# A hybrid decoder layer on one core: first loads, a deferred store, two PSUM tiles, an earlier block load and a halved last store

## The chip, the cores and the metric

The kernel runs on one core of one Trainium2 chip. The metric is the time of one launch in microseconds (us) of device time; three runs of the kernel before gave 2040.29, 2042.28 and 2039.11 us, so its median is 2040.29 us. A core has five engines, each with its own instruction stream: PE (TensorE, matrix products into the PSUM memory), DVE (VectorE), ACT (ScalarE), POOL (GpSimd) and SP (SyncE, which here only issues DMA transfers). PEld is PE's weight load, which overlaps its products. "SPq" and "POOLq" in a profile are the issuing of DMAs on SP and on POOL.

## The reference, cut to what matters

The input is 512 tokens of width 2048, with 16 learned meta tokens set in front. All arithmetic is float32.

```
n = rmsnorm(h) * g_mix;  q, k, v, gb, gc, u = split(n @ w_in)
o_attn = stick_breaking_attention(norm(q), norm(k), v)       # 8 heads of 128
o_conv = gb * causal_dwconv3(gc * u)                         # 1024 channels
h = h + concat(rmsnorm(o_attn), rmsnorm(o_conv)) @ w_out
n2 = rmsnorm(h) * g_ffn
h = h + (silu(n2 @ w_gate) * (n2 @ w_up)) @ w_down           # 5632 wide
return h[meta tokens dropped]
```

## The kernel before, in words

Everything is kept transposed: a tile has 128 channels on its partitions and the tokens along its rows. The matmuls take float32r operands. For float32 accuracy each weight block and each activation block is split into a high and a low part of that type, and a product is three matmuls: high by high, high by low, low by high. The split of a weight block is a CAST on ACT (line 188, the high part) and a subtraction on DVE (line 189, the low part), from the load buffer `w_buf` into the split buffer `s_buf`, which has three places (four for the smaller blocks).

The stages follow one another, and PE is fed without a break from one to the next:

- **The head.** SP issues the vector of gains `vec` (line 72), then by turns pieces of the first weight columns (`load_at`, line 172) and the 16 tiles of x (`load_x`, line 345). Ten small matmuls on ones (line 85) keep PE busy while the loads are under way. `split_x` makes `nh` (ACT, line 351) and `nl` (DVE, line 352) of each x tile, and the k and q products of the first attention head start as soon as the first tile and the first weight piece are split.
- **Attention heads and convolution.** Then comes the rest of w_in.
- **The output projection.** 16 output tiles, of which each takes an attention half (activations `oa`) and a convolution half (`oc`). Each output tile has one PSUM tile `po` with two banks: bank 0 for the attention half, bank 1 for the other (lines 848 to 850 are the three matmuls). In the last two output tiles the attention halves of both are computed first, `attention_half` (line 907) has DVE read bank 0 of each, and only then the convolution halves follow.
- **Gate and up.** 44 pairs (`f`), each computed by `pair_product` in seven block products instead of eight: the blocks x, z, x, z, x, y, x, with y first in the first pair. Between them ACT copies partial sums from PSUM to `sides` (lines 769, 772 and 775), and DVE forms outputs (lines 778, 783 and 788). The third copy, `u2` of line 775, reads x, into which the fifth block (the third on x) then accumulates, so PE must wait for it. `gate` works on the results of a pair while the next pair runs: for even f two combined blocks, for odd f five (`odd`), which `store_acts` splits (ACT and DVE, lines 294 and 295, 1280 columns for odd f) and stores to DRAM as `fd`.
- **Down.** The 22 double blocks of `fd` are taken in four chunks of 4, 6, 6 and 6. For chunk 0 the loop over `j` has four passes of four output tiles; for each later chunk eight passes of two. Each chunk needs seven activation blocks, s = 0 to 6, loaded from `fd` by POOL into `first` (chunk 0) or `ring` (the later chunks). The block products use s = 0, 1, 2, 3, 4, 5, 6 in this order. While chunk 0 is computed, chunk 1 is loaded: blocks 0 and 1 in the second pass, 2 and 3 in the third, 4 and 5 in the fourth, and block 6 in the middle of the fourth, when its place comes free. A load of a block is two DMAs, the high part and the low part, of 768 KB each. So that the loads come no earlier, a tiny POOL operation (line 1074, "TENSOR_SCALAR ring<-d") writes into the place from `last`, an output of the pass before, and the DMAs wait for it. POOL also adds each finished output to DRAM (`add_down`, line 1113, an accumulating DMA "out_T<-d"). In the last chunk the last two output tiles are finished on the core (lines 1170 to 1176) and stored by SP.

A scheduler orders each engine's instructions by priority and by estimated times; `in_turn` stamps some instructions with a token so that they keep the order in which they are written. Each DMA of POOL takes the next of eight semaphores in turn, so that it waits until the DMA eight before it has landed.

Of the kernel before, what the change touches and what calls it, by code (L numbers as in the profile page):

```python
# [33 lines left out]
def hybrid_layer(ctx: ExitStack, tc: tile.TileContext, xT, w_in, w_out, w_gu, w_down, vecs, out):  # L34
# [36 lines left out]
    vec = keep.tile([P, 75], F32, name="vec")  # L71
    nc.sync.dma_start(vec, vecs)
    sc.preload_act_table_set("natural_log_exp_and_others")
# [109 lines left out]
    def split_quad(src, n, turn=False):  # L183
# [6 lines left out]
        split_w.append((hi, lo, n))  # L190

    def in_turn(inst, on=True):
        if on:
            tc.stamp_issue_order_token(inst.ins, "first_pairs")
# [97 lines left out]

    def split(hi, lo, src, eng=ve):
        sc.copy(hi, src)
        eng.tensor_tensor(lo, src, hi.bitcast(F32), ALU.subtract)  # L295
# [73 lines left out]
    for i, (a, b) in enumerate(FIRST):  # L369
        for m in range(2):  # L370
            load_at(HEAD_PLACES[2 * i + m])
            for k in range(len(xts), (a + b) // 2 if m == 0 else b):
                load_x(k)
    for place in HEAD_PLACES[2 * len(FIRST) :]:
        load_at(place)
# [370 lines left out]
    def pair_product(acts, c1, c2, sides, m=1, fourth=None, second=None):  # L746
# [27 lines left out]
        with tc.high_priority(1 << 20):  # L774
            sc.copy(u2, x)  # L775
        block_product(z, acts[3], False, m)
# [115 lines left out]
    def run(steps):  # L892
        for _ in steps:
            pass
# [16 lines left out]
    for i, j in enumerate(OUT_TILES):  # L911
# [5 lines left out]
        if i < KT - 2:  # L917
            hj = attention_half(i, gp if half else ve)
        elif i == KT - 2:
            hs = [attention_half(m, ve) for m in (i, i + 1)]  # L920
        if i >= KT - 2:
            hj = hs[i - KT]
            run(wide_product(ps_out[i][:, 1, :], oc))
        ps = ps_out[i]
        t2 = wide_tmp("t2")
# [4 lines left out]
        def residual(eng):  # L930
            ve.tensor_tensor(t2, ps[:, 1, :], acc_c, ALU.mult)
            eng.tensor_tensor(hj, hj, t2, ALU.add)
            sc.activation(src[:, 2 * half : 2 * half + 2], two(hj), AF.Copy, scale=g_ffn[:, j : j + 1])
# [101 lines left out]

    def store_acts(blks, n, slots, kp):

        t = apool.tile([P, 2, n, T2], F32R, tag=f"s{n}", name=f"s{kp}_{n}")
        split(t[:, 0], t[:, 1], blks)
        c, k = at[kp]  # L1040
        for i, s in enumerate(slots):
            if kp < FT // 2 - 1:
                gp.dma_start(fd[c][s][:, :, k], t[:, :, i])  # L1043
            else:
                nc.sync.dma_start(fd[c][s][:, :, k].bitcast(F32), t[:, :, i].bitcast(F32))
# [3 lines left out]
    def gate(f, g1, u1, x):  # L1049
# [8 lines left out]
        else:  # L1058
# [5 lines left out]
            ve.scalar_tensor_tensor(odd[:, 4], odd[:, 3], -1.0, odd[:, 0], ALU.mult, ALU.subtract)  # L1064
            store_acts(odd, 5, (5, 6, 1, 2, 3), f // 2)

# [64 lines left out]
    for j in range(KT // 4):  # L1131
        for s in ((0, 1), (2, 3), (4, 5))[j - 1] if j else ():
            load_acts(1, s, last)
        c1, c2 = (d, d2)[j % 2][:, 0:2], (d, d2)[j % 2][:, 2:4]
# [13 lines left out]
    for c in range(1, len(CHUNKS)):  # L1148
        end = c == len(CHUNKS) - 1
        for j in range(KT // 2):  # L1150
# [18 lines left out]
            if last_pair:  # L1169
                ve.tensor_tensor(c2, c2, r_h, ALU.mult)  # L1170
                ve.tensor_tensor(c2, c2, h2[1], ALU.add)
                nc.sync.dma_start(two(out[2 * j + 1]), c2)
                ve.tensor_tensor(c1[:, 0], c1[:, 0], r_h[:, 0], ALU.mult)
                ve.tensor_tensor(c1[:, 0], c1[:, 0], h2[0][:, 0], ALU.add)
                ve.tensor_tensor(c1[:, 1], x, r_h[:, 1], ALU.mult)  # L1175
                ve.tensor_tensor(c1[:, 1], c1[:, 1], h2[0][:, 1], ALU.add)  # L1176
                nc.sync.dma_start(two(out[2 * j]), c1)
            else:
                first_sums(2 * j, c1, x, 1)
# [62 lines left out]
```

## Time and profile before

| | |
|---|---|
| median of three runs | 2040.29 us (2039.11 to 2042.28) |
| the profiled execution | 2040.52 us, of which the span from the first to the last instruction is 2038.8 us |
| mean granted TensorE clock over the span | 0.999 |
| HBM traffic | 278.50 MB read, 80.61 MB written |
| DMA q0 (POOL's queue) and q1 (SP's) | 129.65 MB and 229.51 MB |

How to read the lines of the timeline: start in us, duration in us, engine, line of the kernel, operation, "out<-in", the engine's operands and the count of merged instructions; in brackets, how long the engine had been idle and what ended that. A matmul's duration is longer than the distance to the next one, since matmuls are pipelined; the pace is read from start to start. The rows of stages (windows) give the stage, its length, the busy time and count of each engine, the granted PE clock, the mean busy share of the 16 DMA engines (over 1 where transfers overlap) and GB/s. Rows of waits give the engine and line, what it waited for, the total us, the times and the longest. Rows of DMA issues give the transfer, the queue, the count, the size and the time from issue to landing in us.

### The profile page before, as it was taken

The numbers are of one execution on the slowest core, as the hardware profiler recorded it, in microseconds if no ns is written. First come the engines' busy times: TensorE is split into PE (matmuls) and PEld (weight loads), VectorE is DVE, ScalarE is ACT, GpSimd is POOL, SyncE is SP. The second block draws the span as 40 slices with busy tenths as digits, with TensorE's granted clock in tenths as the row PEclk, the third lists the DMA queues.
The fourth block names the chain that finished last, engine by engine and source line by source line (L and its number), as shares of the span: only waits on it lengthen the run. The fifth ranks groups of instructions, "written<-read, shape, count | busy, mean of one in ns | idle before, by whom it ended". The sixth has DMA issues, their size and how long they took to land.

```text
span 2038.8 us, 39740 instructions
## 1 busy us (share of the span) xinstructions
PE 2028.3 (99%) x16158; PEld 1966.2 (96%) x16158; DVE 1721.0 (84%) x2202; ACT 1049.4 (51%) x1517; POOL 381.2 (19%) x532
## 2 busy tenths in 40 slices
PE   9999999999999999999999999999999999999999
PEld 8999999999998889999999999999999999999999
DVE  8788878588977779989989989989989888888887
ACT  7666666344444436455555555555555544444443
POOL 0111111210015440111110110110110252222111
PEclk9999999999999999999999999999999999999999
DMA  6333344753366566555655654554655999989864
GB/s 231 113 117 125 125 137 130 254 146 104 104 219 184 177 189 224 166 163 169 169 162 149 170 164 146 171 161 150 167 161 151 289 305 292 247 236 260 231 152 89
DMA packets 161863, 361.70 MB, mean 177 GB/s; under 512 B 13584, under 2 KB 73488, under 8 KB 161680
## 3 DMA queue, kind: packets, MB, share of 16 engines
q1 hardware_dynamic: 79744, 229.51, 35.4%
q0 software_dynamic: 81936, 129.65, 24.3%
q8 instruction: 127, 2.08, 0.4%
q14 instruction: 56, 0.46, 0.1%
HBM read 278.50 MB, written 80.61 MB: 176 GB/s over the span
## 4 chain that ended last, share of the span: by engine, by line
PE 57%; DMA 1%; issue 1%; DVE 0%; POOL 0%; DVEq 0%; POOLq 0%
PE x L744 32%; PE z L744 16%; PE y L744 8%; DMA ring<-fd 1%; DMA out_T<-d 1%; DVE s_buf L189 0%; POOL out_T L1113 0%; POOL ring L1081 0%; POOL ring L1074 0%; DVE w_buf L201 0%; DVE d L783 0%; DVE d L1121 0%; DVE d L788 0%; DVE d L1175 0%; DVE d L1176 0%
## 5 line engine op out<-in xcount | busy, mean ns | idle before, releaser
L188 ACT CAST s_buf<-w_buf 128x1024 fp32r<-128x1024 f32 (+2 forms) x665 | 659.4, 992 | 759.4 <-PE x L744 369.8
L189 DVE TENSOR_TENSOR s_buf<-w_buf,s_buf 128x1024 fp32r<-128x1024 f32 (+2 forms) x665 | 766.9, 1153 | 127.8 <-ACT s_buf L188 121.5
L744 PE MATMUL x<-f,s_buf 128*128 128x256 f32 x4224 | 500.7, 275 | 0.6 <-ACT sides L775 0.5
L744 PEld LDWEIGHTS x<-f,s_buf 128*128 128x128 f32 x4224 | 488.9, 188 | 1.2 <-ACT sides L775 0.7
L201 DVE TENSOR_TENSOR w_buf<-w_buf 128x1024 f32<-128x1024 f32 (+1 forms) x243 | 278.3, 1145 | 17.2 <-DMA w_buf<-w_in 10.4
L744 PE MATMUL z<-f,s_buf 128*128 128x256 f32 x2112 | 253.6, 275 | 0.0
L744 PEld LDWEIGHTS z<-f,s_buf 128*128 128x128 f32 x2112 | 245.9, 188 | 0.0
L1043 POOL DMA_DIRECT2D fd<-s x147 | 103.6, 921 | 703.9 <-DVE s L295 702.6
L744 PE MATMUL x<-ring,s_buf 128*128 128x256 f32 x1824 | 219.9, 275 | 0.8 <-DMA ring<-fd 0.8
L744 PEld LDWEIGHTS x<-ring,s_buf 128*128 128x128 f32 x1824 | 213.1, 188 | 1.0 <-DMA ring<-fd 1.0
L744 PE MATMUL y<-f,s_buf 128*128 128x256 f32 x1056 | 126.8, 275 | 0.0
L744 PEld LDWEIGHTS y<-f,s_buf 128*128 128x128 f32 x1056 | 123.1, 188 | 0.1
L1113 POOL DMA_DIRECT2D out_T<-d x62 | 60.7, 1014 | 295.2 <-DVE d L1121 227.0
L744 PE MATMUL z<-ring,s_buf 128*128 128x256 f32 x864 | 105.7, 275 | 0.0
L744 PEld LDWEIGHTS z<-ring,s_buf 128*128 128x128 f32 x864 | 101.5, 188 | 0.0
L219 DVE TENSOR_TENSOR w_buf<-w_buf 128x1024 f32<-128x1024 f32 (+1 forms) x81 | 92.3, 1139 | 1.4 <-DMA w_buf<-w_down 1.4
L744 PE MATMUL x<-nh,s_buf 128*128 128x260 f32 x432 | 59.3, 282 | 0.0
L744 PE MATMUL y<-ring,s_buf 128*128 128x256 f32 x432 | 54.5, 279 | 2.2 <-DMA ring<-fd 2.2
L744 PEld LDWEIGHTS x<-nh,s_buf 128*128 128x128 f32 x432 | 55.0, 188 | 0.1
L744 PE MATMUL z<-blk,s_buf 128*128 128x260 f32 x432 | 54.8, 282 | 0.0
L744 PEld LDWEIGHTS y<-ring,s_buf 128*128 128x128 f32 x432 | 52.0, 192 | 2.6 <-issue 1.5
L778 DVE SCALAR_TENSOR_TENSOR gu<-z,sides 128x256 f32<-128x256 f32 x44 | 18.7, 425 | 42.4 <-PE z L744 40.6
(331 smaller groups left out, 3322.3 us busy)
## 6 DMA issues: line engine op xcount, KB each, us to landing
w_buf<-w_gu SPq DMA_DIRECT2D x176, 512.0 KB, 3.4
w_buf<-w_in SPq DMA_DIRECT2D x92, 512.0 KB, 3.4
fd<-s POOLq DMA_DIRECT2D x147, 256.0 KB, 5.3
w_buf<-w_down SPq DMA_DIRECT2D x96, 384.0 KB, 5.0
ring<-fd POOLq DMA_DIRECT2D x42, 768.0 KB, 10.0
w_buf<-w_out SPq DMA_DIRECT2D x32, 512.0 KB, 3.7
out_T<-d POOLq DMA_DIRECT2D x62, 256.0 KB, 5.6
fc<-st SPq DMA_DIRECT2D x8, 1040.0 KB, 6.1
```

The costliest lines, as they stand in the source:

```text
L188: sc.copy(hi, src)
L189: in_turn(ve.tensor_tensor(lo, src, hi.bitcast(F32), ALU.subtract), turn)
L201: in_turn(ve.tensor_tensor(sums[name], a, b, ALU.add), turn)
L219: ve.tensor_tensor(sums["t2"], sums["t2"], b["21"], ALU.add)
L744: pe.matmul(p, wt[:, kk], act(part, k), start=first, stop=wt is lo and k == n - 1, skip_group_check=skip)
L778: in_turn(ve.scalar_tensor_tensor(c2[:, 0], z, -1.0, u2, ALU.mult, ALU.subtract), i == conv_pairs)
L1043: gp.dma_start(fd[c][s][:, :, k], t[:, :, i])
L1113: gp.dma_start(two(out[j]), c, accum_op=ALU.add)
```

## The change

Five edits:

1. In the head, SP's first load is x tile 0, then the first weight piece. `vec` is issued from ACT's queue, ahead of its table load.
2. The split and store of the five odd blocks of f = 1 is put off into the pair f = 2 (`late`), behind the `u2` copy of that pair; a token "third_pair" holds the ACT order of the two.
3. In the last two output tiles of the output projection the convolution halves go to PSUM tiles of their own (`po_c`), each of one bank.
4. Chunk 1's block 0 is loaded in the first pass of chunk 0, without the tiny operation that holds it back; blocks 1 and 2 come in the second pass, 3 and 4 in the third, 5 in the fourth.
5. The very last store is two, one for each half of the tokens, the first issued before the second half is computed.

```diff
-    nc.sync.dma_start(vec, vecs)
+    sc.dma_start(vec, vecs)
...
+    late = []
+
+    def in_order(inst, on):
+        if on:
+            tc.stamp_issue_order_token(inst.ins, "third_pair")
...
-    def split(hi, lo, src, eng=ve):
-        sc.copy(hi, src)
+    def split(hi, lo, src, eng=ve, turn=False):
+        in_order(sc.copy(hi, src), turn)
         eng.tensor_tensor(lo, src, hi.bitcast(F32), ALU.subtract)
...
         for m in range(2):
-            load_at(HEAD_PLACES[2 * i + m])
+            if i or m:
+                load_at(HEAD_PLACES[2 * i + m])
             for k in range(len(xts), (a + b) // 2 if m == 0 else b):
                 load_x(k)
+            if not (i or m):
+                load_at(HEAD_PLACES[0])
...
         block_product(x, acts[2], False, m)
         with tc.high_priority(1 << 20):
-            sc.copy(u2, x)
+            in_order(sc.copy(u2, x), i == conv_pairs + 2)
+        if late:
+            late.pop()()
         block_product(z, acts[3], False, m)
...
+        conv_half = ps_out[i][:, 1, :]
         if i >= KT - 2:
-            hj = hs[i - KT]
-            run(wide_product(ps_out[i][:, 1, :], oc))
-        ps = ps_out[i]
+            hj, conv_half = hs[i - KT], small(f"po_c{i}")
+            run(wide_product(conv_half, oc))
...
         def residual(eng):
-            ve.tensor_tensor(t2, ps[:, 1, :], acc_c, ALU.mult)
+            ve.tensor_tensor(t2, conv_half, acc_c, ALU.mult)
...
-    def store_acts(blks, n, slots, kp):
+    def store_acts(blks, n, slots, kp, turn=False):
...
-        split(t[:, 0], t[:, 1], blks)
+        split(t[:, 0], t[:, 1], blks, turn=turn)
...
-            store_acts(odd, 5, (5, 6, 1, 2, 3), f // 2)
+            if f == 1:
+                late.append(lambda: store_acts(odd, 5, (5, 6, 1, 2, 3), 0, True))
+            else:
+                store_acts(odd, 5, (5, 6, 1, 2, 3), f // 2)
...
     for j in range(KT // 4):
-        for s in ((0, 1), (2, 3), (4, 5))[j - 1] if j else ():
-            load_acts(1, s, last)
+        for s in ((0,), (1, 2), (3, 4), (5,))[j]:
+            load_acts(1, s, last if j else None)
...
                 ve.tensor_tensor(c1[:, 0], c1[:, 0], h2[0][:, 0], ALU.add)
+                nc.sync.dma_start(out[2 * j][:, :T2], c1[:, 0])
                 ve.tensor_tensor(c1[:, 1], x, r_h[:, 1], ALU.mult)
                 ve.tensor_tensor(c1[:, 1], c1[:, 1], h2[0][:, 1], ALU.add)
-                nc.sync.dma_start(two(out[2 * j]), c1)
+                nc.sync.dma_start(out[2 * j][:, T2:], c1[:, 1])
```

Three places show how the instructions move. Names are those of the program with a buffer number; a line number is that of each kernel's own file, which is why the same operation has another one.

POOL's queue in the first and second pass of chunk 0, before: `first` are chunk 0's blocks, `ring` a place of the ring, `fd_0`, `fd_1` the blocks 0 and 1 of chunk 1, `out_T` the accumulating stores.

```order
L1081 DMA first_17365<-fd_6_7970 128x2x512 x2
L1113 DMA out_T<-d 256x1x256
L1074 TENSOR_SCALAR ring_17397<-d 128x2
L1074 TENSOR_SCALAR ring_17398<-d 128x2
L1081 DMA ring_17397<-fd_0_7971 128x2x768
L1113 DMA out_T<-d 256x1x256 x2
```

The same place after:

```order
L1095 DMA first_17367<-fd_6_7972 128x2x512 x2
L1095 DMA ring_17399<-fd_0_7973 128x2x768 x2
L1127 DMA out_T<-d 256x1x256
L1088 TENSOR_SCALAR ring_17400<-d 128x2 x2
L1095 DMA ring_17400<-fd_1_7974 128x2x768
L1127 DMA out_T<-d 256x1x256 x2
```

Block 0 now stands right behind chunk 0's own loads, ahead of the first accumulating store, and block 1 has moved into the place that block 0 had.

POOL's queue in the fourth pass, before; `fd_6`, `fd_4` and `fd_5` are the blocks 6, 4 and 5 of chunk 1.

```order
L1074 TENSOR_SCALAR ring_17398<-d 128x2 x2
L1081 DMA ring_7922<-fd_6_7977 128x2x768
L1113 DMA out_T<-d 256x1x256
L1081 DMA ring_17398<-fd_4_7975 128x2x768 x2
L1081 DMA ring_17398<-fd_5_7976 128x2x768 x2
```

The same place after:

```order
L1088 TENSOR_SCALAR ring_17400<-d 128x2
L1095 DMA ring_7924<-fd_6_7979 128x2x768
L1127 DMA out_T<-d 256x1x256
L1095 DMA ring_17400<-fd_5_7978 128x2x768 x2
```

Block 5 now stands where block 4 stood; block 4 has gone into the third pass.

ACT in the pair f = 2, before: the copies to `sides` are lines 769, 772 and 775 of the kernel before, "CAST s_5" is the split of the five odd blocks, "CAST s_buf" that of a weight block.

```order
L769 COPY sides<-x_8437 128x256
L188 CAST s_buf<-w_buf 128x1024
L772 COPY sides<-z_8436 128x256
L294 CAST s_5_8427<-odd_8422 128x1280
L188 CAST s_buf<-w_buf 128x1024
L775 COPY sides<-x_8437 128x256
```

The same place after:

```order
L778 COPY sides<-x_8431 128x256
L188 CAST s_buf<-w_buf 128x1024
L781 COPY sides<-z_8430 128x256
L188 CAST s_buf<-w_buf 128x1024
L784 COPY sides<-x_8431 128x256
L300 CAST s_5_8514<-odd_8424 128x1280
```

The long CAST of the odd blocks stood two rows ahead of the third copy and now stands behind it.

## The prediction

> **What bounds the kernel now.** I read the page first, then the busy time by stages, the waits of PE, and the timeline around each wait. The page's first part says that PE has work for 99% of the span:
>
> ```profile
> PE 2028.3 (99%) x16158; PEld 1966.2 (96%) x16158; DVE 1721.0 (84%) x2202; ACT 1049.4 (51%) x1517; POOL 381.2 (19%) x532
> ```
>
> PE is the bound, and its number of products does not change. Time can only come from places where PE stands still or runs slowly. Two stretches of equal length, the second with the change of chunk in the down product:
>
> ```profile
> 1400.00:1600.00 200.00, 200.00 (x1767) 200.00 (x1767) 179.58 (x201) 104.35 (x140) 28.89 (x41) 1.00 0.56 163
> 1600.00:1800.00 200.00, 196.98 (x1719) 196.41 (x1718) 171.56 (x222) 92.08 (x126) 62.81 (x76) 0.99 1.00 283
> ```
>
> The second holds 48 products fewer (1719 against 1767, at 200/1767 = 0.113 us each: 5.4 us lost), and its DMA engines are busy throughout. PE's waits between 1690 and 1710 us name the cause:
>
> ```profile
> PE y L744 <- DMA ring<-fd: 2.2, 2, 1.3
> PE x L744 <- DMA ring<-fd: 0.8, 1, 0.8
> ```
>
> **The change part by part.** *Chunk 1's early load* comes first, since it is the largest term. PE in the first pass of chunk 1:
>
> ```profile
> 1692.67 2.20 PE L744 MATMUL z<-ring,s_buf 128*128 128x256 f32 x18
> 1694.71 0.84 PE L744 MATMUL x<-ring,s_buf 128*128 128x256 f32 x6
> 1696.35 1.68 PE L744 MATMUL x<-ring,s_buf 128*128 128x256 f32 x12 [0.79 <-DMA ring<-fd]
> 1699.33 0.94 PE L744 MATMUL y<-ring,s_buf 128*128 128x256 f32 x6 [1.30 <-DMA ring<-fd]
> 1701.19 2.91 PE L744 MATMUL y<-ring,s_buf 128*128 128x256 f32 x12 [0.92 <-DMA ring<-fd]
> 1708.39 2.20 PE L744 MATMUL z<-ring,s_buf 128*128 128x256 f32 x18
> ```
>
> A block of 18 products takes 1694.71 - 1692.67 = 2.04 us. From 1694.71 to 1708.39 stand four blocks (x, y, x and the next pass's x), 8.16 us of work in 13.68 us: 5.5 us lost. Part of it is a slower clock (the column behind POOL's), right after the waits:
>
> ```profile
> 1701.00:1705.00 4.00, 3.81 (x19) 3.81 (x20) 0.79 (x1) 0.84 (x1) 1.88 (x4) 0.57 1.18 253
> ```
>
> That is 4 x (1 - 0.57) = 1.7 us; the other 3.8 us are the waits. A rule of the Trainium skill speaks against counting the 1.7 us in: "TensorE: Matmul & The Clock Gate", section "What's actually happening", has the clock halve after an idle window of some 3.4 us. By that rule these waits, 1.3 us at most, would not cause it, and 3.8 us would be the whole term; the row disagrees, since the drop begins where they end and stretches without waits read 1.00. I count 5.5 and keep 3.8 as a rival.
>
> Who was late? POOL issued the last three loads here, and these are two of the times from issue to landing (of the load at 1676.72, then of that at 1683.19):
>
> ```profile
> 1676.72 2.57 POOL L1081 DMA_DIRECT2D ring<-fd  x2
> ...
> 1683.19 0.71 POOL L1081 DMA_DIRECT2D ring<-fd  x1 [2.12 <-DMA out_T<-d]
> ```
>
> ```profile
> ring<-fd POOLq DMA_DIRECT2D x1, 768.0 KB, 17.5
> ```
>
> ```profile
> ring<-fd POOLq DMA_DIRECT2D x1, 768.0 KB, 18.0
> ```
>
> The first is the high part of block 4 (landing 1676.72 + 17.5 = 1694.2), the last the low part of block 5 (1683.19 + 18.0 = 1701.2, where the last wait ends). The low part of block 4 landed where x went on, at 1696.3. After the change, POOL's order is the same up to here but with one block less behind it: block 5 has the two slots that block 4 had, so its parts land at about 1694.2 and 1696.3. Without waits, y starts at 1694.71 + 2.04 = 1696.75 and needs the low part 6/18 of a block later, at 1697.4. The margins are 2.5 and 1.1 us, and block 4 comes with the third pass's loads. So all waits go, the last by a narrow margin.
>
> Is there room for block 0 where it goes? The DMA engines before and after the second pass's loads begin (the last but one column is their share):
>
> ```profile
> 1630.00:1636.00 6.00, 6.00 (x55) 6.00 (x54) 6.00 (x8) 3.07 (x4) 2.90 (x2) 1.00 0.58 135
> 1636.00:1700.00 64.00, 61.91 (x544) 61.54 (x542) 57.81 (x74) 28.66 (x35) 29.77 (x35) 1.00 1.14 333
> ```
>
> Yes: the engines move 333 GB/s when pressed and 135 just before, so block 0's 1.5 MB (4.7 us at 333) fits largely into that slack, which is 1.2 MB in these six us alone. Behind its issue POOL holds only the accumulating store that waits for DVE anyway. Term: **-5.5 us**, bounds -6 and 0.
>
> *The deferred split.* In the pair f = 2:
>
> ```profile
> 814.95 2.88 PE L744 MATMUL x<-f,s_buf 128*128 128x256 f32 x24
> ...
> 817.67 2.88 PE L744 MATMUL z<-f,s_buf 128*128 128x256 f32 x24
> ...
> 818.50 1.27 ACT L294 CAST s<-odd 128x1280 fp32r<-128x1280 f32 x1 [2.94 <-DVE odd L1064]
> 819.68 1.04 ACT L188 CAST s_buf<-w_buf 128x1024 fp32r<-128x1024 f32 x1
> ...
> 820.63 0.36 ACT L775 COPY sides<-x 128x256 f32<-128x256 f32 x1
> ...
> 821.04 3.02 PE L744 MATMUL x<-f,s_buf 128*128 128x256 f32 x24 [0.49 <-ACT sides L775]
> ...
> 826.34 0.42 DVE L783 SCALAR_TENSOR_TENSOR gu<-x,sides 128x256 f32<-128x256 f32 x1
> ...
> 826.90 5.73 PE L744 MATMUL x<-f,s_buf 128*128 128x256 f32 x48
> ...
> 832.47 2.88 PE L744 MATMUL z<-f,s_buf 128*128 128x256 f32 x24
> ```
>
> A block here takes 817.67 - 814.95 = 2.72 us. From 817.67 to 832.47 are five, 13.6 us in 14.8: 1.2 us lost. The `u2` copy could have run once its x was done at about 817.7, but ACT had waited for the odd blocks, spent 1.27 us on them and 1.04 us on a weight. DVE then ran late too, so that line 783 freed x only at 826.76. With the copy ahead, x can start at 820.39. The odd blocks' split costs ACT and DVE the same as before, later, where ACT has idle time (51% busy); DVE, with its 1280 columns a weight later, is the one that could be late next. Term: **-1.2 us**, bounds -1.3 and +0.5.
>
> *The own PSUM tiles.*
>
> ```profile
> 758.57 0.39 PE L848 MATMUL po<-oa,s_buf 128*128 128x512 f32 x1
> ...
> 758.92 0.68 DVE L907 TENSOR_TENSOR w<-po,acc_a 128x512 f32<-128x512 f32 x1
> 759.03 0.39 PE L850 MATMUL po<-oa,s_buf 128*128 128x512 f32 x1
> ...
> 759.75 0.47 PE L848 MATMUL po<-oc,s_buf 128*128 128x512 f32 x1 [0.34 <-ACT st L294]
> ```
>
> The pace is (759.03 - 758.57)/2 = 0.23 us; the first `oc` product comes 0.72 us after its forerunner. It goes on just after DVE's read of the same tile's other bank ends (759.60), so I take the read as the cause, not the ACT instruction that the row names; the new tile has no such reader. Term: **-0.5 us**, bounds -0.6 and 0.
>
> *The first loads.*
>
> ```profile
> 0.82 0.38 SPq L72 DMA_DIRECT2D vec<-vecs  x1
> ...
> 1.14 4.24 PE L85 MATMUL warm<-ones 128*128 128x128 f32 x20 [1.14 <-DVE one L81]
> ...
> 1.73 0.42 SPq L345 DMA_DIRECT2D xt<-xT  x1
> ...
> 4.81 0.73 ACT L351 ACTIVATE nh<-xt,vec 128x528 fp32r<-128x528 f32 x1 [0.73 <-DMA xt<-xT]
> ...
> 5.60 0.51 PE L280 MATMUL pk<-nh,s_buf 128*128 128x264 f32 x2 [0.23 <-ACT nh L351]
> ```
>
> The x tile lands 4.81 - 1.73 = 3.1 us after its issue; issued at 0.82 it is there at 3.9, and `vec`, from ACT at about the same time and far smaller, before it. `nh` (0.73) and the weight's CAST, now behind it (about 0.4), end at 5.0, against 5.54 now. The warm-up products end at 5.38, so PE's own start moves by about 0.3, but ACT and DVE, which PE waits for in the next 10 us, are about 0.5 ahead. Term: **-0.4 us**, bounds -1.0 (all loads one issue earlier) and +0.3 (another order of casts in the head).
>
> *The halved last store.*
>
> ```profile
> 2035.90 0.34 SPq L1177 DMA_DIRECT2D out_T<-d  x1
> ```
>
> ```profile
> out_T<-d SPq DMA_DIRECT2D x1, 256.0 KB, 2.0
> ```
>
> The second half is issued at the same moment with half the bytes; the first is on its way while DVE computes the second. Of 2.0 us, the part that goes with size is at most half of it. Term: **-0.3 us**, bounds -0.8 and 0. The Trainium skill, "DMA: Bandwidth & Descriptors", section "Anatomy of one DMA", gives a fixed 2.0 us plus bytes at 436 GB/s; by it, as an estimate, half of 256 KB saves 0.3 us, while its whole, 2.6 us, is more than the 2.0 of this row.
>
> The sum is -5.5 - 1.2 - 0.5 - 0.4 - 0.3 = **-7.9 us**. The profiled execution took 2040.52 us (span 2038.8 and 1.7 around it) and would take 2032.6; it stands 0.2 above the median, which goes from 2040.29 to **2032.4 us**.
>
> **The rivals.** *The loads stay late* (0.14). The DMA engines are at 1.14 of their share all the way from 1636 to 1700, and the low part of block 5 has a margin of only 1.1 us. If DMA as a whole and not the order sets the landing, PE waits again and its clock drops again: the 5.5 us stay and the time is 2040.3 - 2.4 = 2037.9. Against it: 1.5 MB leave this stretch.
>
> *The clock drops anyway* (0.06), as the rule above would have it: 2032.4 + 1.7 = 2034.1.
>
> *Waits in other places* (0.08). DVE is nearly full in the pair f = 2, and the head has a new order; if these two gain nothing, 2032.4 + 1.6 = 2034.0. That is also what comes if the tokens don't hold what they should.
>
> *Block 0 starves the weights, slower* (0.04). In the first pass its 1.5 MB compete with SP's weight loads. Two of these, issued at 1601.14 under chunk 0's own loads and at 1622.5 after them, took:
>
> ```profile
> w_buf<-w_down SPq DMA_DIRECT2D x1, 512.0 KB, 12.8
> ```
>
> ```profile
> w_buf<-w_down SPq DMA_DIRECT2D x1, 512.0 KB, 6.1
> ```
>
> Even 12.8 us made PE wait for nothing. Weights are split about two blocks of 2.72 us ahead, so PE would begin to wait near 12.8 + 5.4 = 18 us, each us costing one, and 1.7 us for the clock. At 26 us the time is 2032.4 + 8 + 1.7 = 2042.1. From 6.1 us, block 0's 4.7 us bring it to about 11, which is short of the point.
>
> **How the numbers follow.** The forecast has 0.68. The range goes from 2030.8 (head and last store at their better bounds, -1.1, and a part of the scatter of the three runs, 3.2 us) to 2036.0, which takes in the clock, the other waits and, with the scatter, half of the first rival's 5.5 us, and leaves out the first rival and the slower one. A measurement of this kernel can tell about 0.2% or 4.1 us from no change. Faster than 2036.2 are forecast, clock and other waits: 0.68 + 0.06 + 0.08 = 0.82. The first rival (0.14) and half of the last (0.02) are within 0.2%, 0.16; slower, 0.02.
>
> **What would show it.** Right: no wait of PE for `ring<-fd`, a clock of 1.00 from 1690 to 1710, block 5's two parts landing 17 to 20 us after the issue of the first; the odd CAST behind the third copy and x on time in the pair f = 2; no gap before the first `oc` product of the last two tiles; the first product near 5.3 us; the last landing 0.3 us earlier behind its issue. Wrong: a wait for `ring<-fd` or for `w_buf` between the 1610th and the 1710th us, or a clock drop without a wait.

## The result, and the profile after

Median of six runs: 2034.81 us (2033.44 to 2035.44), beside 2040.99 us for the kernel before (median of six). The ratio is 0.9968, with a 95% interval of 0.9956 to 0.9979: a gain of 6.2 us, where 7.9 were forecast. The profiled execution took 2035.44 us, of which 2033.7 are the span. Five executions beside the experiments below, three of them of the kernel before, took over 140 us longer than the rest of their kernel; the medians hardly move by them, and the counts and intervals leave them out.

The largest term is there. The stretch with the change of chunk and the 20 us behind the old waits, by windows (start and end, length, the busy time and count of PE, PEld, DVE, ACT and POOL, then the granted clock, the DMA share and GB/s):

```profile
1600.00:1800.00 200.00, 199.99 (x1765) 199.79 (x1764) 176.19 (x229) 94.40 (x128) 63.25 (x76) 1.00 1.03 293
1690.00:1710.00 20.00, 20.00 (x178) 20.00 (x178) 17.75 (x27) 9.73 (x15) 7.21 (x8) 1.00 1.14 313
```

PE now does 1765 products in the 200 us (1719 before), at a clock of 1.00 throughout. The timeline of PE in the first pass of chunk 1:

```profile
1693.00 2.20 PE L753 MATMUL z<-ring,s_buf 128*128 128x256 f32 x18
1695.04 2.20 PE L753 MATMUL x<-ring,s_buf 128*128 128x256 f32 x18
1697.08 2.20 PE L753 MATMUL y<-ring,s_buf 128*128 128x256 f32 x18
```

The blocks follow one another every 2.04 us, with no wait for `ring<-fd`. What the loads did in the fourth pass: first POOL's issue of block 5's two parts in the timeline, then the view of these two by tile (durations in ns, first and last start, and the times from issue to landing in us), then the list of DMA issues for the second of them:

```profile
1676.90 2.59 POOL L1095 DMA_DIRECT2D ring<-fd  x2
```

```profile
L1095 POOL DMA_DIRECT2D ring<-fd x2: 1854/1856/1858, 1676.9 to 1677.6; - x2
DMA to landing us min/median/max: 16.8/17.7/18.5
```

```profile
ring<-fd POOLq DMA_DIRECT2D x1, 768.0 KB, 18.5
```

The high part, issued at 1676.9, took 16.8 us and landed at 1693.7. The low part, issued at 1677.6, landed at 1696.1. PE needs it at 1697.08 + 0.68 = 1697.76, so it had 1.6 us to spare; 1.1 were forecast.

The pair f = 2, timeline of ACT and of PE:

```profile
818.18 1.06 ACT L188 CAST s_buf<-w_buf 128x1024 fp32r<-128x1024 f32 x1 [1.40 <-PE x L753]
819.14 0.36 ACT L784 COPY sides<-x 128x256 f32<-128x256 f32 x1
819.52 1.27 ACT L300 CAST s<-odd 128x1280 fp32r<-128x1280 f32 x1
```

```profile
818.89 2.88 PE L753 MATMUL z<-f,s_buf 128*128 128x256 f32 x24
821.61 2.88 PE L753 MATMUL x<-f,s_buf 128*128 128x256 f32 x24
824.33 2.88 PE L753 MATMUL y<-f,s_buf 128*128 128x256 f32 x24
827.05 3.22 PE L753 MATMUL x<-f,s_buf 128*128 128x256 f32 x27
```

The third copy now stands ahead of the long CAST, and PE starts a block every 2.72 us without a wait. In the output projection, the timeline of PE around the first `oc` product:

```profile
759.60 0.39 PE L861 MATMUL po<-oa,s_buf 128*128 128x512 f32 x1
759.83 0.39 PE L859 MATMUL po_c<-oc,s_buf 128*128 128x512 f32 x1
```

The distance is 0.23 us, PE's pace, where it was 0.72.

Three things were not as forecast. The head: ACT's timeline after the start.

```profile
4.07 0.73 ACT L357 ACTIVATE nh<-xt,vec 128x528 fp32r<-128x528 f32 x1 [1.53 <-DMA vec<-vecs]
...
7.00 0.73 ACT L357 ACTIVATE nh<-xt,vec 128x528 fp32r<-128x528 f32 x1 [1.06 <-DMA xt<-xT]
```

The first `nh` begins 0.74 us earlier than before (4.81), but ACT then waits for the second x tile until 7.00 (before, the second `nh` began at 6.29). The first product on `pv`, the end of the head, came at 30.51 us against 29.77 (timeline of PE, before and then after):

```profile
29.77 0.51 PE L280 MATMUL pv<-nh,s_buf 128*128 128x264 f32 x2 [0.31 <-ACT tmp L458]
```

```profile
30.51 0.49 PE L286 MATMUL pv<-nh,s_buf 128*128 128x264 f32 x2
```

Second, a new wait in the first pair of gate and up:

```profile
784.34 1.07 PE L753 MATMUL x<-f,s_buf 128*128 128x256 f32 x8
786.43 2.13 PE L753 MATMUL x<-f,s_buf 128*128 128x256 f32 x16 [1.02 <-DMA f<-fx]
```

PE waits for an activation block that is loaded back from DRAM; it costs 1.2 us beside the pace. Third, the end: timeline of SP's last store, and its row in the list of DMA issues (the two halves).

```profile
2030.71 0.33 SPq L1192 DMA_DIRECT2D out_T<-d  x1
```

```profile
out_T<-d SPq DMA_DIRECT2D x2, 128.0 KB, 1.7
```

The landing is 0.3 us shorter, but from the issue to the end of the span it is 2033.7 - 2030.71 = 3.0 us, where it was 2038.8 - 2035.90 = 2.9.

Setting each product of PE against the same product in the trace of before gives the account of the profiled pair: +0.6 us up to the output projection (+0.7 at the end of the head), -0.6 there, +1.2 for `f<-fx`, -1.2 in f = 2, +0.3 near 1621 us (a late copy on ACT), -5.5 at the change of chunk and +0.1 at the end: about -5.1 in all.

### The profile page after: what moved, and what is told of

The parts are those of the page before. It is cut to its first block, busy times and chain, and to the rows that moved or that the text cites. A ratio compares the mean times of both kernels' runs of the same rounds, so it can differ in the third digit from the quotient of the medians.

```text
span 2033.7 us, 39736 instructions
## 1 busy us (share of the span) xinstructions
PE 2025.3 (100%) x16158; PEld 1964.0 (97%) x16158; DVE 1721.2 (85%) x2202; ACT 1050.1 (52%) x1517; POOL 382.1 (19%) x531
## 4 chain that ended last, share of the span: by engine, by line
PE 96%; DVE 1%; DMA 1%; ACT 1%; issue 0%; POOL 0%; SPq 0%; DVEq 0%; ACTq 0%
PE x L753 40%; PE z L753 20%; PE y L753 10%; PE po L859 3%; PE po L860 3%; PE po L861 3%; PE pv L286 1%; PE pv L288 1%; PE pv L290 1%; PE pk L286 1%; PE pk L288 1%; PE pk L290 1%; PE pq L290 1%; PE pq L286 1%; PE pq L288 1%; PE pcu L286 1%
## 5 line engine op out<-in xcount | busy, mean ns | idle before, releaser
L286 PE MATMUL pk<-nh,s_buf 128*128 128x264 f32 x256 | 52.9, 288 | 0.9 <-ACT nh L357 0.8
L753 PEld LDWEIGHTS z<-blk,s_buf 128*128 128x128 f32 x432 | 53.1, 188 | 0.0
```

The costliest lines, as they stand in the source:

```text
L286: pe.matmul(ps, wh, ah[:, a:b], start=k == 0, stop=False)
L753: pe.matmul(p, wt[:, kk], act(part, k), start=first, stop=wt is lo and k == n - 1, skip_group_check=skip)
```

## The experiments

Theory A of the head, at this point, was that the new order of the first loads makes it late; theory B, that the DMA engines had a slow moment in that one execution. Times of kernels that were run together are compared with each other and with the kernel before beside them.

### The change once more

No edit.

> The changed kernel once more, as the base of the head experiments. In its first profile the head came out 0.7 us late: the first product began at 5.15 us (5.60 before), but the first product on pv at 30.51 (29.77 before), and a new wait of 1.2 us for f<-fx stood at 785. Theory A (the new order of the first loads makes the head late): the first product on pv begins at 30.3 to 30.7 again. Theory B (the DMA engines had a slow moment in that one execution): it begins at 29.3 to 29.6, 0.2 to 0.5 ahead of the kernel before, since the first product keeps its lead. Time 2034.8 by A, about 2033.8 by B. The wait for f<-fx: 1.0 to 1.4 us again if PE's earlier arrival in that stage causes it, under 0.5 if one slow load did.

2033.98 us against 2040.86, ratio 0.9969 [0.9957, 0.9981]. ACT's second `nh` in its timeline:

```profile
6.41 0.74 ACT L357 ACTIVATE nh<-xt,vec 128x528 fp32r<-128x528 f32 x1 [0.59 <-DMA xt<-xT]
```

`pv` began at 29.89, between what the two theories gave; the second tile was again waited for, but for less. The wait for `f<-fx` was absent, and PE's x block there began at 783.98 and ran through. Of the ten later traces that have the third edit, and of the two without it, none shows that wait: it belongs to one execution in which those loads were slow (the last two of them took 8.2 us in the median from issue to landing, 6.3 in this run).

### The head, one half of the edit at a time

The change without its first edit:

```diff
-    sc.dma_start(vec, vecs)
+    nc.sync.dma_start(vec, vecs)
...
-            if i or m:
-                load_at(HEAD_PLACES[2 * i + m])
+            load_at(HEAD_PLACES[2 * i + m])
...
-            if not (i or m):
-                load_at(HEAD_PLACES[0])
```

> The change without its first edit: vec is SP's first load again, then the weight piece, then x tile 0. Theory A (the new order makes the head late): first product at 5.6 us, first product on pv at 29.8, and 0.7 us less time than the changed kernel. Theory B (chance): first product on pv at 29.8 too, but the changed kernel beside it at 29.3 to 29.6, and 0.2 to 0.5 us more time than it.

Only `vec` on ACT's queue (the second and third hunk above alone):

> The change with half of its first edit: vec is issued from ACT's queue, but SP's first loads are the weight piece and then x tile 0, as before. If vec from ACT's queue is what comes late (in the first profile of the changed kernel nh waited for vec until 4.07 us, 3.2 us after its issue, where the kernel before had it 1.8 us after its issue from SP): vec lands near 4.1 us again, x tile 0 near 4.4 (issued one step earlier than before), nh begins near 4.4, the first product near 5.2 and the first product on pv at 29.4 to 29.6, earlier than before by the one step. If instead three queue entries at once slow the DMA engines, pv begins at 30.3 or later here too.

Only the order of x and weight (the first hunk alone):

> The change with the other half of its first edit: vec is SP's first load, as before, then x tile 0, then the weight piece. If the order of x and weight is what makes the head late, the first product on pv begins at 30.3 to 30.7 here too, and PE shows the same wait for nh of the second x tile (0.8 us in the changed kernel). If vec on ACT's queue is the cause, vec lands at 2.6 us, nh begins near 4.3, and pv begins at 29.8 or before, with 0.7 us less time than the changed kernel.

Times: 2034.56, 2034.09 and 2034.67 us, beside 2033.98 for the whole change; the four agree within 0.7, less than the runs of one kernel differ. `pv` began at 30.45, 30.11 and 30.91, none of them where it was expected. The old order, then, came out at 30.45 here and at 29.77 in the kernel before, with the same loads: B holds for the difference between executions, and no gain of the new order over the old is seen. What hardly changes is ACT's way from the second `nh` on. From its start to the end of the sixteenth it takes 24.52 - 6.29 = 18.2 us in the kernel before, 25.11 - 7.00 = 18.1 in the change, 24.53 - 6.41 = 18.1 in the repeat and 25.42 - 7.30 = 18.1 with the order alone. With `vec` alone moved it is 18.4. It is longer where a later load is late too: 19.0 in the run with the old order, where a load held ACT for 0.56 us at 9.92. `pv` follows 5.2 to 5.5 us behind. In these traces, then, the head counts from the second x tile and from late loads behind it, and not from the first tile.

### The fourth edit alone, and the change without it

```diff
-        for s in ((0, 1), (2, 3), (4, 5))[j - 1] if j else ():
-            load_acts(1, s, last)
+        for s in ((0,), (1, 2), (3, 4), (5,))[j]:
+            load_acts(1, s, last if j else None)
```

Added to the kernel before:

> The kernel before with the fourth edit alone (chunk 1's block 0 in the first pass, two blocks in the second, two in the third, one in the fourth). Theory A (what made PE wait was that the fourth pass carried two blocks and a half; one block less there is enough): no wait for ring<-fd, granted clock 1.00 from 1690 to 1710 us, 5.5 us less than the kernel before, 2035.4 against 2040.9. Theory B (the landings are set by the DMA engines' load as a whole, and the other edits, which bring PE there earlier or later, had a part in it): a wait of 0.5 us or more for ring<-fd stays, and the gain is under 4 us.

Taken out of the change:

> The change without its fourth edit: chunk 1's blocks are loaded as in the kernel before. Theory A: three waits for ring<-fd of 0.8 to 1.3 us each and a clock near 0.57 in the 4 us behind them come back, 5.5 us in all, 2039.4 against 2034.0 for the whole change. Theory B (as above): the waits differ by over 1 us in sum from the 3.0 us of the kernel before.

The edit alone: 2036.06 us against 2040.41, ratio 0.9975 [0.9966, 0.9985], and no wait for `ring<-fd`. Its window:

```profile
1690.00:1710.00 20.00, 20.00 (x179) 20.00 (x178) 17.78 (x27) 9.64 (x17) 7.60 (x9) 1.00 1.09 291
```

So the mechanism is A's. The gain in the medians is 4.4 us and not 5.5; the interval of the ratio, 3.1 to 6.9 us, holds both. Without the edit: 2037.67 us against the same 2040.41, so the other four edits gain 2.7. The whole change gained 6.2 and 6.9 against the kernel before beside it, which leaves 3.4 to 4.1 for the fourth edit. In the profiled execution without it, PE's one wait and the windows around it:

```profile
1697.92 1.66 PE L753 MATMUL y<-ring,s_buf 128*128 128x256 f32 x12 [1.88 <-DMA ring<-fd]
```

```profile
1695.00:1700.00 5.00, 3.12 (x26) 2.84 (x25) 3.27 (x6) 1.20 (x2) 2.14 (x4) 1.00 1.17 268
1700.00:1705.00 5.00, 5.00 (x47) 5.00 (x46) 4.51 (x7) 1.95 (x3) 1.14 (x2) 1.00 1.16 267
```

One wait of 1.9 us, and the clock stays at 1.00: neither the three waits nor the drop of the kernel before, so here it is B's sign that came. The 5.5 us, then, are one execution's. The runs of the kernel before that stand beside all these experiments show how common its case is: of 78, 45 had a mean granted clock of 0.999 or less and a median of 2041.0 us, 33 had 1.000 and 2039.3. The difference is 1.8 us, about the 1.7 that the prediction had read from the drop. Where the clock fell in these runs is not on record, only its mean. If it is this drop, it comes in about 6 of 10 executions and not in all, which takes 0.42 x 1.7 = 0.7 us off the term.

### Where must the bytes go: out of the fourth pass, or out of the whole stretch?

Blocks 4 and 5 both in the fourth pass again, block 0 still in the first:

```diff
-        for s in ((0,), (1, 2), (3, 4), (5,))[j]:
+        for s in ((0,), (1, 2), (3,), (4, 5))[j]:
```

> The change with blocks 4 and 5 both in the fourth pass again, block 3 alone in the third, block 0 in the first as in the change. It tells whether the bytes that leave the whole stretch (block 0's 1.5 MB) or the bytes that leave the fourth pass make the gain. Theory A (the fourth pass's queue decides): blocks 4 and 5 land as in the kernel before, the last part near 18 us after its issue, waits of 2.5 to 3.5 us in sum for ring<-fd, then a clock near 0.57, and nearly all of the 5.5 us are lost: 2039 to 2040. Theory B (the load of the stretch as a whole decides): with 1.5 MB less in the stretch, 4.7 us of the engines' time at 333 GB/s, block 5 lands 2 to 5 us earlier than in the kernel before, waits under 1 us, and 2034 to 2035.5.

Block 0 not in the first pass but in the second, the fourth pass as in the change:

```diff
-        for s in ((0,), (1, 2), (3, 4), (5,))[j]:
+        for s in ((), (0, 1, 2), (3, 4), (5,))[j]:
```

> The change with block 0 not in the first pass but in the second, ahead of blocks 1 and 2; two blocks in the third and one in the fourth, as in the change. The first pass's free DMA time goes unused. Theory A (the fourth pass's queue decides): no wait for ring<-fd, as in the change, 2034 to 2034.5. Theory B (the load of the stretch from 1636 to 1700 as a whole decides): the 1.5 MB are back in it, block 5's low part lands 2 to 5 us later than in the change, PE waits 1.5 us or more and its clock drops: 2036 to 2040.

2038.50 and 2038.99 us: neither is better than the run without the fourth edit, 2037.67 us beside them. PE's waits of the first, then of the second:

```profile
PE y L753 <- DMA ring<-fd: 2.5, 2, 1.3
```

```profile
PE y L753 <- DMA ring<-fd: 2.4, 2, 1.3
```

The first experiment is nearer to A (the fourth pass decides; the clock of its profiled execution stayed at 1.00, though), the second is B's (the whole stretch decides), so neither theory holds alone: the change needs both. POOL's timeline in the fourth pass of the second experiment:

```profile
1673.45 1.35 POOL L1095 DMA_DIRECT2D ring<-fd  x1
...
1676.86 0.74 POOL L1095 DMA_DIRECT2D ring<-fd  x1 [0.93 <-DMA ring<-fd]
1680.38 0.73 POOL L1095 DMA_DIRECT2D ring<-fd  x1 [2.78 <-DMA ring<-fd]
```

POOL has to wait for earlier loads to land before it may issue the two parts of block 5: the second goes out at 1680.38, in the change at 1677.6. But that alone does not make them late. The first part goes out at 1676.86, as in the change (1676.90), and still takes 2.5 us longer (list of DMA issues, this run and then the change):

```profile
ring<-fd POOLq DMA_DIRECT2D x1, 768.0 KB, 19.3
```

```profile
ring<-fd POOLq DMA_DIRECT2D x1, 768.0 KB, 16.8
```

The second part, issued 2.8 us later than in the change, lands 18.1 us behind its issue, 2.4 later than in the change and so no later than the first. What was issued ahead of the two is still under way: block 0, pushed into the second pass, has moved the backlog into the fourth. Windows of the stretch ahead of it, of the change and then of the kernel before, show that block 0 uses room that was there:

```profile
1615.00:1636.00 21.00, 20.99 (x185) 20.79 (x185) 20.66 (x24) 11.35 (x13) 4.00 (x4) 1.00 1.09 357
```

```profile
1615.00:1636.00 21.00, 21.00 (x187) 21.00 (x187) 20.66 (x25) 11.43 (x13) 2.90 (x2) 1.00 0.93 286
```

(357 - 286) GB/s x 21 us = 1.5 MB, the size of the block. The weight load issued at 1622.83 in it took 8.4 us (6.1 before), and no product waited for one.

### Another head, and a whole last store

```diff
-            if i or m:
+            if i:
                 load_at(HEAD_PLACES[2 * i + m])
...
-            if not (i or m):
-                load_at(HEAD_PLACES[0])
+            if not i:
+                load_at(HEAD_PLACES[m])
...
-                nc.sync.dma_start(out[2 * j][:, :T2], c1[:, 0])
...
-                nc.sync.dma_start(out[2 * j][:, T2:], c1[:, 1])
+                nc.sync.dma_start(two(out[2 * j]), c1)
```

> The change with two edits that the traces so far point to. SP's loads begin with x tile 0, weight piece 0, x tile 1, weight pieces 1 and 2 (in the change x tile 1 stands behind weight piece 1), and the last store is one of 256 KB again, in place of two halves. Theory A on the head (ACT works without a pause from the second x tile to about 26 us, so the landing of that tile sets the time of all that follows, and the first tile does not): the second nh begins at 5.5 to 6.2 us instead of 6.4 to 7.3, and the first product on pv by as much earlier, at 29.0 to 29.6 instead of 29.9 to 30.9. Theory B (the DMA engines' pace over the first 16 us sets it, in whatever order): the first product on pv begins at 29.9 to 30.9 as in the other kernels. On the store: if halving it gains the 0.3 us of the shorter landing, the time from the last product's start to the end of the span is 4.5 here, against 4.2 in the change; if it gains nothing, since something follows the landing, it is 4.1 as in the kernel before. In all 2033.5 to 2034.0 by A, 2034.0 to 2034.6 by B.

2034.11 us against 2040.05, ratio 0.9974 [0.9964, 0.9984]. The second `nh` began at 6.23, at the edge of what A gave, and the first product on `pv` at 30.18, which is B's value, though the earlier second tile that A starts from hardly came. That tile, issued at 1.73 in place of 2.20, took 4.5 us to land (3.0 for the first one), so that it landed at 6.21, within the 6.10 to 6.98 of the traces with the change's order: moving it one place ahead did little. On the store, the last issue and its time to landing:

```profile
2028.99 0.34 SPq L1191 DMA_DIRECT2D out_T<-d  x1
```

```profile
out_T<-d SPq DMA_DIRECT2D x1, 256.0 KB, 2.0
```

The span ends at 2031.9, 2.9 us behind the issue, as in the kernel before, and 4.15 us behind the start of the last product; with the halves it was 3.0, and 4.24 to 4.33 in all ten traces that have them. Halving gains nothing.

### The second and the third edit taken out

```diff
-            if f == 1:
-                late.append(lambda: store_acts(odd, 5, (5, 6, 1, 2, 3), 0, True))
-            else:
-                store_acts(odd, 5, (5, 6, 1, 2, 3), f // 2)
+            store_acts(odd, 5, (5, 6, 1, 2, 3), f // 2)
```

> The change without its second edit: the odd blocks of f = 1 are split at once again. If the term was sized rightly, the waits of PE in the pair f = 2 come back (0.5 us for sides and some 0.7 us of slower starts), the shift of PE's products between 815 and 833 us against the kernel before is 0 instead of -1.2, and the time is 1.2 us above that of the whole change, 2035.3 to 2035.8. If the drained pair were late for another reason (DVE, full in this stretch), the shift is -0.5 or more in amount here too.

2035.19 us, 1.1 above the kernel of the last section, which ran beside it (single runs of one kernel differ by over 2 us). The wait is back (timeline of PE), and the shift against the kernel before does not change between 815 and 833 us:

```profile
820.86 3.04 PE L753 MATMUL x<-f,s_buf 128*128 128x256 f32 x24 [0.48 <-ACT sides L784]
```

```diff
-            hj, conv_half = hs[i - KT], small(f"po_c{i}")
+            hj = hs[i - KT]
```

> The change without its third edit: the convolution halves of the last two output tiles go to bank 1 of the tile whose bank 0 DVE reads. If the term was sized rightly, the gap of 0.5 us ahead of the first oc product comes back and the time is 0.5 us above the whole change. On the wait for f<-fx at 785 us, 1.2 us in the changed kernel's first profile and absent in its repeats: if PE's earlier arrival made it, the wait stays under 0.5 here; if it is the chance of one slow load, it is absent here too and proves nothing for the edit, and the time stays 0.5 above.

2034.51 us, 0.4 above the same kernel; the first `oc` product again comes 0.72 us behind its forerunner, so the wait goes with the tile, and in the traces both terms have their forecast size.

```profile
760.70 0.39 PE L861 MATMUL po<-oa,s_buf 128*128 128x512 f32 x1
761.42 0.47 PE L859 MATMUL po<-oc,s_buf 128*128 128x512 f32 x1 [0.34 <-ACT st L300]
```

The row names a CAST on ACT, the prediction DVE's read of the other bank. The trace of the change tells them apart (DVE's read and ACT's CAST at the same place):

```profile
759.50 0.68 DVE L918 TENSOR_TENSOR w<-po,acc_a 128x512 f32<-128x512 f32 x1
759.61 0.62 ACT L300 CAST st<-src 128x512 fp32r<-128x512 f32 x1 [3.21 <-DVE src L955]
```

There the first `oc` product starts at 759.83, while both are still running, to 760.18 and 760.23. So it does not need the CAST; what the third edit took away is the tile that it shared with the read.

### Less work for ACT in the head

```diff
             s = t512(L, "r", 3)
-            sc.activation(s, xts[k], AF.Square)
+            if k % 2:
+                gp.tensor_tensor(s, xts[k], xts[k], ALU.mult)
+            else:
+                sc.activation(s, xts[k], AF.Square)
```

> The change with the last store whole and, in the head, the squares of seven of the sixteen x tiles (the odd ones from the third on) made on POOL, which stands idle there, in place of ACT (0.55 us each). The tiles' sums are the same; the scheduler moves other instructions too, behind the head above all, so the head is read from the trace and the time only beside it. In all the kernels so far ACT took 18.1 us from the start of the second nh to the end of the last (plus 0.5 to 0.7 where a load came late), and the first product on pv began 5.2 to 5.5 us behind that, at 29.8 to 30.9, whatever the order of the first loads. Theory A (ACT's work sets the head, and so an earlier first tile could not): with 7 x 0.55 = 3.9 us less on ACT the last nh ends 1.0 us or more sooner after the second one begins (under 17.1 us), and the first product on pv begins before 29.3. Theory B (DVE, busy for 18.7 of the 20 us from 5 to 25, or the loads, at 387 GB/s there, set it just as much): 17.5 us or more, and pv at 29.6 or later. DVE's own operations slower by a tenth or more beside POOL's would speak for B.

The last store is whole here too. 2039.89 us, 0.9995 [0.9985, 1.0005] of the kernel before: most of the gain is gone. The sixteenth `nh` ends 19.8 us behind the start of the second one, and the first product on `pv` starts at 33.24 us, 3.4 later than in the repeat of the change; by 60 us PE is 5.8 us late. Neither of A's two signs came. DVE's timeline, then POOL's:

```profile
8.26 0.42 DVE L189 TENSOR_TENSOR s_buf<-w_buf,s_buf 128x256 fp32r<-128x256 f32 x1
...
9.72 1.29 DVE L189 TENSOR_TENSOR s_buf<-w_buf,s_buf 128x256 fp32r<-128x256 f32 x1
```

```profile
9.16 1.57 POOL L367 TENSOR_TENSOR tmp<-xt 128x528 f32<-128x528 f32 x1 [7.52 <-DMA xt<-xT]
```

A DVE operation that takes 0.42 us elsewhere takes 1.29 beside POOL's, and ACT now waits for DVE (2.4 us in the head, 0.6 in the repeat). The Trainium skill, "SBUF — State Buffer", section "SBUF: two separate sides", says that GpSimd and VectorE share a pair of ports, and that of a GpSimd operation that reads SBUF and a VectorE operation with two SBUF inputs the one that starts first holds the pair for its whole instruction. The trace agrees: POOL's runs from 9.16 to 10.73, and DVE's, on two inputs, ends 0.3 us after it. So the run brought a cost of its own and does not decide between A and B: whether ACT's work, DVE's or the loads hold the head without this collision stays open.

## Why the prediction was right or wrong

- **The early load.** Mechanism, places and landing times were right: 1693.7 and 1696.1 for 1694.2 and 1696.3, no wait, a mean clock of 1.000 in all twelve runs of the change. The low part had 1.6 to 2.5 us to spare in the ten traces with this edit as it stands. The step that failed is the size: the term was taken from one profiled execution of the kernel before, 5.5 us. It is 5.5 in the profiled pair too, but 4.4 in the medians alone and 3.4 to 4.1 as a part of the whole, since the waits and the drop differ from execution to execution.
- **The drop of the clock.** It comes behind these waits and went with them; the rival in which it stays did not occur. But gaps alone do not tell when it comes: gaps of 1.1, 1.6 and 1.2 us between products' starts brought it in the kernel before, and gaps of 1.4 and 1.5 in the run with blocks 0 to 2 in the second pass; gaps of 1.5 and 1.6 in the run with blocks 4 and 5 in the fourth did not, nor did one of 2.2 in the run without the fourth edit. The traces show more. In the records of the granted clock of all fourteen, each stretch at one clock that ends within the execution is a whole number of steps of 3.41 us, and each of the two drops behind these waits is one step at half the clock, which costs 1.7 us. The steps before and at the drop, first of the kernel before, then of the run with blocks 0 to 2 in the second pass (windows, PE's busy time first):

```profile
1697.84:1701.25 3.41, 1.19 (x9) 0.83 (x7) 2.76 (x4) 0.39 (x1) 1.00 (x2) 1.00 1.20 296
1701.25:1704.66 3.41, 3.41 (x16) 3.41 (x17) 0.45 (x1) 0.84 (x1) 1.63 (x3) 0.50 1.19 241
```

```profile
1695.70:1699.11 3.41, 1.51 (x10) 1.33 (x11) 2.48 (x4) 0.00 (x0) 1.19 (x3) 1.00 1.18 241
1699.11:1702.52 3.41, 3.41 (x18) 3.41 (x17) 1.38 (x3) 0.83 (x1) 1.44 (x2) 0.50 1.17 270
```

The emptiest step among the waits in each of the two runs without a drop (blocks 4 and 5 in the fourth pass, then no fourth edit):

```profile
1697.13:1700.54 3.41, 1.84 (x13) 1.66 (x14) 1.83 (x3) 0.00 (x0) 1.85 (x3) 1.00 1.20 235
```

```profile
1694.03:1697.44 3.41, 2.02 (x16) 1.66 (x14) 3.41 (x7) 0.84 (x1) 0.00 (x0) 1.00 1.15 326
```

PE was busy for 1.19 and 1.51 us of the step ahead of a drop, and for 1.84 and 2.02 where none followed. At the end of each execution, where PE runs out of work, the clock falls behind the first step with 0.5 us or less; the emptiest step that no drop followed, in the last steps of the run without the fourth edit, has 1.53. So what fits all fourteen traces is that the clock is halved for a step when PE stood idle for some 1.9 us or more of the 3.41 before it; like waits then bring it or not by how the steps cut them. This is read from the traces and no run tested it, and the limit is rough, since the ends of products are modelled. The Trainium skill, "TensorE: Matmul & The Clock Gate", section "What's actually happening", adds that the window in which idleness is counted runs freely. The traces agree: from the span's start, a step begins at 4.83 us in the kernel before and at 6.10 in the second of these runs. Steps that fall differently in each execution would fit the 45 of 78, though no run here shows that.
- **The first rival** (the loads stay late) did not occur, and the two runs that moved one block back show how near it was: either half of the edit undone brings it back.
- **Block 0 starves the weights** did not occur: 8.4 us, where I had worked out about 11 and put the point of waiting near 18.
- **The deferred split and the PSUM tiles** were right in mechanism and in size: 1.2 and 0.5 us in the traces. The medians have 1.1 and 0.4, which their scatter alone would not show. DVE did not come late in f = 2.
- **The first loads.** The step that failed is "ACT and DVE, which PE waits for in the next 10 us, are about 0.5 ahead". They were ahead for one tile. I had looked at when the first tile lands and taken the second one for granted. Over the seven traces with the change's first loads, `pv` begins at 29.83 to 30.51, 30.13 in the mean; over the three with the old ones at 29.77, 30.45 and 30.66, 30.29 in the mean. That is 0.2 us at most, in a scatter of 0.7 to 0.9, and the profile of before was the best of its three.
- **The halved last store.** The step that failed is that a shorter landing ends the span sooner. The landing was 0.3 us shorter, as sized, but the end came 0.1 later; what follows the landing is not in the trace. The fit of the Trainium skill, "DMA: Bandwidth & Descriptors", section "Anatomy of one DMA", which the prediction set beside its term, is given there for DMAs issued by GpSimd, and this store is SP's: by the fit, as an estimate, 256 and 128 KB would take 2.6 and 2.3 us; measured were 2.0 and 1.7.
- **The sum.** Each against the kernel before beside it, the fourth edit alone gains 4.4 us and the other four alone 2.7 (2.4 had been counted), together 7.1; measured for the whole were 6.2 and 6.9. The median of the kernel before moved by 0.9 us between these sets of runs (2040.05 to 2040.99), so the parts add up no closer than that. Of the 1.0 to 1.7 us that are missing from 7.9, 0.7 had been counted for the head and the store, of which no trace shows a gain; the rest lies in the early load. The time came out 2.4 us above the forecast and inside the range, but not by the ways for which the range's upper part had been kept: the clock did not drop, and the deferred split gained what it should. That it lies within is in part luck. No kernel here beats the change by more than the scatter.

## What to carry to other kernels

When several loads queue behind busy DMA engines, look at all that is issued ahead of the last one: here, moving one load to where the engines had room and taking one out of the last pass helped together, and with either undone the wait was back. A stall that is read from one execution should be priced from several: the mean clock of the other runs told here that the dear case was 6 of 10. Short waits that stand close together can cost more than their sum: here they brought 3.41 us at half the clock, 1.7 us more. Before moving the first load of a pipeline ahead, look at what waits for the second.

## What the runs showed that I had not expected

- `vec`, 37.5 KB, landed 3.0 to 3.2 us after its issue from ACT's queue with an x tile issued at the same moment (2.6 with a weight piece), and 1.7 to 1.8 us after its issue from SP with nothing issued at the same moment. Queue and company were not told apart.
- An x tile of 264 KB took 2.8 to 3.0 us where it was the first load. In the traces with the change's first loads the second x tile took 3.9 to 4.8, with other loads in flight.
- A DVE subtraction of 128x256 took 1.29 us beside a POOL product, against 0.42 without it.
- The span ended 1.3 us behind the last landing with two half stores and 0.9 behind a whole one.
